# Columns of the second layer's scale and shift by transpositions, and 128 score columns for its first token tile

## The chip, the cores and the metric

The kernel runs on one core of one Trainium2 chip. The core has engines that run side by side: TensorE (PE, matrix products, with its weight loads PEld), VectorE (DVE), ScalarE (ACT), GpSimd (POOL), and SyncE (SP), which issues most of the transfers. The metric is the device time of one execution in microseconds, lower being better. Of several executions the median is given. The profile is of one more execution.

## What is computed

Two layers over 256 tokens of 1024 numbers, batch one. Each layer scales and shifts its normalized input by vectors that depend on a condition `c`, projects it, attends, gates the result and projects it back:

```python
cond = jax.nn.silu(c)
for i in range(DEPTH):
    shift, scale, gate = jnp.split(cond @ ada_w[i] + ada_b[i], 3, axis=-1)
    h = rms_norm(x, norm_g[i]) * (1 + scale[:, None, :]) + shift[:, None, :]
    ...
    x = x + gate[:, None, :] * y
```

The first layer's mixer (`nsa_mixer`) adds three attentions: over compressed blocks, over selected blocks and over a window. The second layer's (`moba_mixer`) is, at this length, plain causal attention, as its one block of 256 holds all tokens:

```python
s_own = jnp.einsum('bcgrd,bkgd->bcgrk', qc, k_own) * scale
...
p = masked_softmax(s_own, m_own).astype(v.dtype)
return jnp.einsum('bcgrk,bkgd->bcgrd', p, v_own)
```

There are 16 query heads of 64 and 4 key heads; a key head serves four query heads. All data are float32.

## The kernel before

**Products.** A weight or an activation is split in two fp32r parts, hi and lo, and a product is the sum of hi x hi, hi x lo and lo x hi, one pass each. The tokens are two tiles of 128 (`m` = 0 and 1). The normalized, scaled and shifted input stands transposed in `HT` (1024 features in eight groups of 128), so the scale and the shift are needed as columns, one number per partition and feature group: `AB[l]`.

**Scale and shift (`ada_rows`, `ada_ss`).** `ada_rows` multiplies the condition with the weights' columns. In `condz` only the first of each 32 columns holds the condition, the others are zero; four tiled products at a time put their results in PSUM rows 0 and 32 (the shift: even and odd feature groups of the condition) and 64 and 96 (the scale, likewise). All rows but these four are zero. The result is copied to `g` in SBUF, a tile "row". `ada_ss` turns these rows into columns and adds each pair: for each of the `nk` groups of 128 features, `g` is the stationary operand of a float32 product with `selP`, a 128x2 matrix with ones in rows 0 to 63 of its first column and in rows 64 to 127 of its second. Two additions and one fused step on VectorE then make `AB[l]`. The first layer does this in pieces of one or two groups (`nk` = 1, 2), the second layer in two pieces of four, which run as steps of the list `side` during the first layer's attention (`beside()` calls one step). The second layer's columns are first used in `next_h`, which makes the second layer's input after the first layer's output product.

**Second layer's attention (`pair_b`).** Eight pairs of heads. For each pair and each token tile `m`, `scores` computes two heads' scores against all 256 keys, keys split in hi and lo (`KTB`, a view of the tile KTA), with queries of one 128-token tile as the stationary operand: four products for each `m`. Of tile 0 only the first 128 keys are read by what follows (`masked_top`, which adds the causal mask and takes the row maximum); `exps`, the division, the transposition (`p_transposed`) and the product with the values follow, then `gated` with the `zT` columns.

**The order.** Nothing is issued as it stands in the code. `Plan` records each instruction, or each `plan.group()` of them, with what it reads and writes and a cost (`_cost`), and `issue` then simulates the engines and puts each engine's instructions in order by when they could start, by level (`FIRST_OF_ALL`, `URGENT`, `CHAIN`, `FILL`) and by which buffers are free. Tiles come from tags with a fixed number of buffers ("ps": six PSUM banks, "ss": four small SBUF tiles). Weight products are `FILL` and so stand between the attention's steps. PE's costs are in cycles, divided by 2.4 or 1.2 to get ns:

```python
if method == "transpose":
    return 262.0 if aps[1].dtype == F32 else 180.0
...
    return 2 * max(cols * 2.14, 264.0)
return max(cols * (1.07 if aps[2].dtype == F32R else 1.0), 264.0)
```

The third line is for a plain float32 product, the last for fp32r. As all instructions are issued from one place in `issue`, most rows of the profile show line L373; tile names tell them apart (`ps<-selP,row` is the product with `selP`, `ps<-KTA,qg` are scores, `row`, `AB` and `ss` are the tiles above).

Of the kernel before, what the change touches and what calls it, by code (L numbers as in the profile page):

```python
# [14 lines left out]
OP = mybir.AluOpType  # L15
AX = mybir.AxisListType

P = 128
# [382 lines left out]
def kernel(  # L401
# [29 lines left out]
    T, A, V, G, Q = plan.T, plan.A, plan.V, plan.G, plan.S  # L431
    tile_of = plan.tile
# [69 lines left out]
    identF = const.tile([P, P], F32, name="identF")  # L502
# [6 lines left out]
    selP = const.tile([P, 2], F32, name="selP")  # L509
# [130 lines left out]
    def ada_rows(l, cs, n, loaded=None):  # L640

        acc = tile_of("ps", 512)
        step = min(1024 // n, 4)
        level = plan.level if loaded else FILL
        for kk in range(8):
            if kk % step == 0:
                w = loaded[kk // step] if loaded else [ada_piece(l, kk, c0, n) for c0 in cs]
            run = max(step, 2) if n > P else 4
            if kk % run == run - 1:
                with plan.at(level), plan.group():  # L650
                    for k in range(kk - run + 1, kk + 1):
                        for s in range(2):
                            j = s * 2 + k % 2
                            T.matmul(acc[32 * j:32 * j + 32, :n], condz[:, k, :], w[s][:, k % step, :],
                                     start=(k < 2), stop=(k >= 6), tile_position=(0, 32 * j))
            if kk % step == step - 1 and kk < 7:
                yield
        g = tile_of("row", n)
        if n == P:
            V.tensor_copy(g, acc[:, :n])  # L660
        else:
            A.copy(g, acc[:, :n])
        return g
# [3 lines left out]
    def ada_ss(l, k0, nk, loaded=None):  # L667

        g = yield from ada_rows(l, (k0 * P, D + k0 * P), nk * P, loaded)
        t = tile_of("ps", 512)  # L670
        with plan.group():
            for q in range(nk):
                T.matmul(t[:, 2 * q:2 * q + 2], g[:, q * P:(q + 1) * P], selP, start=True, stop=True)
        tv = t[:, 0:2 * nk].rearrange("p (q s) -> p q s", s=2)
        b = ROW_ADA + 24 * l + k0
        a_, b_ = AB[l][:, 0, k0:k0 + nk], AB[l][:, 1, k0:k0 + nk]
        if nk == 1:
            V.tensor_scalar(a_, tv[:, :, 1], RT1[:, b + 8:b + 9], RT[:, ROW_G + 8 * l + k0:ROW_G + 8 * l + k0 + 1],
                            op0=OP.add, op1=OP.mult)
            V.tensor_add(b_, tv[:, :, 0], RT[:, b:b + nk])  # L680
            return
        V.tensor_add(a_, tv[:, :, 1], RT[:, b + 8:b + 8 + nk])
        V.scalar_tensor_tensor(a_, a_, 1.0, RT[:, ROW_G + 8 * l + k0:ROW_G + 8 * l + k0 + nk], op0=OP.add, op1=OP.mult)
        V.tensor_add(b_, tv[:, :, 0], RT[:, b:b + nk])
# [169 lines left out]
    def scores(q, kt, g, k0, n, need):  # L854

        s = tile_of("ps", 2, 256)
        with plan.group(need):
            for e in range(2):
                T.matmul(s[:, e, 0:n], q[e], kt[:, 0, g, k0:k0 + n], start=(e == 0), stop=False)
                T.matmul(s[:, e, 0:n], q[e], kt[:, 1, g, k0:k0 + n], start=False, stop=(e == 1))  # L860
        return s
# [4 lines left out]
    def masked_top(dst, src, neg, at):  # L866

        mask = causal[:, P - at:P - at + src.shape[-1]]
        V.tensor_tensor_reduce(dst, src, mask, -1.0, 3.0e38, op0=OP.add, op1=OP.min, accum_out=neg)

    def exps(dst, bias, total):
        A.activation(dst, dst, AF.Exp, bias=bias, scale=-1.0, accum_out=total)

    def inverse(sm):
        V.tensor_scalar_max(sm, sm, 1e-30)
        V.reciprocal(sm, sm)

    def p_transposed(block):

        pT = []  # L880
        for e in range(2):
            t = tile_of("ps", 512)
            with plan.group():
                for j in range(3):
                    T.transpose(t[:, j * P:(j + 1) * P], block(e, j), identF)
            s = tile_of("pT", 384)
            A.copy(s, t[:, 0:384])
            pT.append(s)
        return pT

    def values(o, parts, first):

        with plan.group():
            for n, (v, pT) in enumerate(parts):
                for e in range(2):
                    T.matmul(o[64 * e:64 * e + 64, 0:S], v[0], pT[e][:, 0:S], start=(first and n == 0), stop=False,
                             tile_position=(0, 64 * e))
                for e in range(2):
                    T.matmul(o[64 * e:64 * e + 64, P:S], v[1], pT[e][:, S:S + P], start=False,
                             stop=(n == len(parts) - 1), tile_position=(0, 64 * e))  # L900
# [3 lines left out]
    def gated(i, o, zT):  # L904
        t = tile_of("g", S)
        V.scalar_tensor_tensor(t, zT, 0.5, o[:, :S], op0=OP.mult, op1=OP.mult)
        if i % 2 == 0:
            pair = tile_of("qg", 2, 2, S)
            GT[i], GT[i + 1] = pair[:, 0], pair[:, 1]
        A.copy(GT[i][:, 0, :], t)  # L910
        V.tensor_sub(GT[i][:, 1, :], t, GT[i][:, 0, :].bitcast(F32))
# [53 lines left out]
    for m in range(2):  # L965
        xm, ss = tile_of("n_in", D), tile_of("ss", 16)[:, 0:1]
# [4 lines left out]
        for q in range(2):  # L971
            sl = slice(512 * q, 512 * q + 512)
            t = tile_of("ps", 4, P)
# [87 lines left out]
    for k in range(2):  # L1061
# [7 lines left out]
        with plan.at(URGENT):  # L1069
            for m in range(2):  # L1070
# [3 lines left out]
                h = tile_of("rot", P)  # L1074
# [6 lines left out]
        for m in range(2):  # L1081
            for ci, ((hi, lo), sl) in enumerate(w):
                acc = kv_acc[ci][m]
                with plan.at(FILL):
                    for i, (half, part) in enumerate(((0, hi), (0, lo), (1, hi))):
                        T.matmul(acc, HT[:, half, k, m * P:(m + 1) * P], part[:, sl],
                                 start=(k == 0 and i == 0 and (ci < 3 or m == 0)), stop=False, skip_group_check=True)

    for at, (what, k0, *rest) in enumerate(START):
        load_stage(what, k0, *rest)  # L1090
        if at == TABLES:
            TCS, NBc, TC, TR, TS = tables()
        if what == "s":
            nk = rest[0]
            with plan.at(URGENT):
                at_once(ada_ss(0, k0, nk, loaded[k0]))
                hv = xT[k0 // 4][:, k0 % 4:k0 % 4 + nk, :]
                for k in range(nk):
                    affine(HT[:, 0, k0 + k], hv[:, k, :], 0, k0 + k, A)
                    h = tile_of("rot", S)  # L1100
                    affine(h, hv[:, k, :], 0, k0 + k, V)
                    V.tensor_sub(HT[:, 1, k0 + k], h, HT[:, 0, k0 + k].bitcast(F32))
        else:
            for ci in range(4):
                w = parts_of(kv_w[k0][ci])
                for m in range(2):
                    product(kv_acc[ci][m], k0, m, w, of_h)
# [26 lines left out]
    for kv in range(2):  # L1134
        for m in range(2):
            t = tile_of("ps", 512)
# [3 lines left out]
            tv = t.rearrange("p (g u r e) -> p e r g u", g=KVH, r=8, e=2)  # L1140
# [22 lines left out]

    hid = tile_of("ps", 512)
    side += [cmp_steps(hid), ada_gate(0), ada_ss(1, 0, 4), ada_ss(1, 4, 4)]
    QT = qt_tiles()
    gates = const.tile([P, 2, HEADS, 3], F32, name="gates")
# [36 lines left out]
    with plan.group():  # L1204
        for cc in range(2):
            T.matmul(cmp_ps[0:64, 0:64], u[:, cc, 0, :], w2[:, 0, cc, :], start=(cc == 0), stop=(cc == 1))
        for m in range(2):
            T.matmul(cmp_ps[0:64, 64:96], selC[:, m].rearrange("p g n -> p (g n)"), TCS[:, m, :],
                     start=(m == 0), stop=(m == 1))
# [22 lines left out]
    for hf in range(2):  # L1232
        for cc in range(2):
# [4 lines left out]
                     start=(cc == 0), stop=(cc == 1))  # L1238
# [169 lines left out]
    KTB = KTA.rearrange("p a g k -> p (a g k)")[:, 0:2048].rearrange("p (a g k) -> p a g k", a=2, g=KVH)  # L1408
# [22 lines left out]
    def pair_b(i):  # L1431
        g = i // 2
        pm = [tile_of("p", 2, P), tile_of("p", 2, 256)]
        neg, sm = tile_of("tiny", 2, 2), tile_of("tiny", 2, 2)
        for m in range(2):
            n = P * (m + 1)
            q = [QT[g][:, 2 * (i % 2) + e, m * P:(m + 1) * P] for e in range(2)]
            s = scores(q, KTB, g, 0, 256, pm[m])
            for e in range(2):
                masked_top(pm[m][:, e], s[:, e, 0:n], neg[:, m, e:e + 1], m * P)  # L1440
            for e in range(2):
                exps(pm[m][:, e], neg[:, m, e:e + 1], sm[:, m, e:e + 1])
        inverse(sm.rearrange("p m e -> p (m e)"))
        for m in range(2):
            for e in range(2):
                V.tensor_scalar_mul(pm[m][:, e], pm[m][:, e], sm[:, m, e:e + 1])
        pT = p_transposed(lambda e, j: pm[0][:, e] if j == 0 else pm[1][:, e, (j - 1) * P:j * P])
        o = tile_of("ps", 512)
        vs = slice(g * HD, (g + 1) * HD)
        values(o, [([VB[:, m, vs] for m in range(2)], pT)], True)  # L1450
        gated(i, o, zT[i])

    for i in range(8):
        pair_b(i)
        beside()
# [37 lines left out]
```

## Time and profile before

| | |
|---|---|
| three runs, us | 319.18, 318.23, 319.22; median 319.18 |
| profiled execution, us | 318.98 |
| its span, first to last instruction, us | 317.3 |
| mean granted TensorE clock | 0.998 |
| HBM read | 64.36 MB |
| transfers' mean rate over the span | 207 GB/s |

How to read the profile: the page gives each engine's busy time and share of the span; "slices" cut the span into 40 parts, with the busy share in tenths. A group row has line, engine, operation, output and input tiles, shapes and count, then busy time in us and the mean length of one in ns, then idle time ahead of it. A timeline row has start, length, engine, the same names and a count, with idle time ahead of it in brackets. Records of PE overlap, since products are pipelined: a row's length is that of all its records together, from the first start to the last end. The chain of work that ended last is followed back from the end; its rows have start, length and what ran.

### The profile page before, as it was taken

The page shows a single profiled execution, that of the slowest core. Times are in us where ns is not written, and L with a number is a line of the kernel's source. Part 1 is how long each engine was busy: PE and PEld are TensorE (multiplying, and loading weights), DVE is VectorE, ACT ScalarE, POOL GpSimd, SP SyncE. Part 2 cuts the span into 40 slices and gives each one's busy share as a digit, 9 for nine tenths or more (in the row PEclk, how much of TensorE's full clock was granted, in tenths as well). Part 3 has the DMA queues.
Part 4 walks back from the last instruction along what each step waited for, and adds up shares of the span by engine and source line. Part 5 has one row for each costly group of instructions (what it writes and reads, how often), then busy time and mean ns, then how long its engine had stood idle before and what let it go on. Part 6 is the DMA issues. An engine that isn't in the chain of part 4 may idle for free.

```text
span 317.3 us, 6173 instructions
## 1 busy us (share of the span) xinstructions
PE 307.2 (97%) x2141; PEld 245.2 (77%) x2141; DVE 241.6 (76%) x732; ACT 205.2 (65%) x486; POOL 26.5 (8%) x102
## 2 busy tenths in 40 slices
PE   4999999999999999999999999999999999999995
PEld 4666677777766797868888988877788999968784
DVE  4663374669983899835979877997599999999763
ACT  5635155765835887456799856786586489998520
POOL 8138910000000000000000000000000000000000
PEclk9999999999999999999999999999999999999999
DMA  8999999359898813787274447727278872524002
GB/s 252 320 357 365 368 359 320 98 161 348 272 308 285 300 53 126 236 303 242 92 265 133 135 134 223 240 62 210 68 257 270 285 238 74 161 73 133 35 34 102
DMA packets 44174, 65.82 MB, mean 207 GB/s; under 512 B 4221, under 2 KB 20971, under 8 KB 44142
## 3 DMA queue, kind: packets, MB, share of 16 engines
q1 hardware_dynamic: 43782, 65.36, 63.8%
q8 instruction: 17, 0.28, 0.4%
q14 instruction: 15, 0.12, 0.1%
q10 hardware_dynamic: 168, 0.06, 0.1%
q0 software_dynamic: 192, 0.00, 0.0%
HBM read 64.36 MB, written 1.05 MB: 206 GB/s over the span
## 4 chain that ended last, share of the span: by engine, by line
PE 82%; DVE 7%; DMA 5%; ACT 3%; issue 2%; ACTq 0%; SPq 0%; DVEq 0%
PE ps L373 49%; PE acc L373 33%; DVE lo L373 3%; ACT hi L373 2%; DMA raw<-in_ada_w_dram 2%; DMA y<-in_ada_b_dram 2%; DMA early<-in_nsa_w_in_dram 1%; DVE n_out L373 1%; DVE gate L373 1%; DVE rs L373 0%; ACT n_in L373 0%; DVE p L373 0%; DVE ss L373 0%; DVE zT L373 0%; ACT p L373 0%
## 5 line engine op out<-in xcount | busy, mean ns | idle before, releaser
L373 DVE TENSOR_TENSOR lo<-raw,hi 128x1024 fp32r<-128x1024 f32 (+1 forms) x48 | 56.4, 1181 | 11.0 <-ACT hi L373 10.8
L373 ACT CAST hi<-raw 128x1024 fp32r<-128x1024 f32 (+1 forms) x48 | 48.9, 1022 | 23.1 <-DMA raw<-in_nsa_w_in_dram 8.3
L373 PE MATMUL acc<-hi,HT 128*128 128x512 f32 (+1 forms) x160 | 49.6, 381 | 1.5 <-ACT n_in L373 0.8
L373 ACT ACTIVATE p<-p,tiny 128x128 f32<-128x128 f32 (+1 forms) x96 | 43.0, 456 | 8.3 <-DVE tiny L373 8.2
L373 PE MATMUL acc<-HT,hi 128*128 128x256 f32 x192 | 37.7, 285 | 0.0
L373 PEld LDWEIGHTS acc<-hi,HT 128*128 128x128 f32 x160 | 29.0, 188 | 9.8 <-issue 2.9
L373 DVE CUSTOM_DVE_ANT_0 p<-ps,causal 128x128 f32<-128x128 f32 (+1 forms) x96 | 30.8, 345 | 3.5 <-PE ps L373 3.4
L373 PEld LDWEIGHTS acc<-HT,hi 128*128 128x128 f32 x192 | 30.1, 188 | 0.6 <-issue 0.6
L373 PE MATMUL acc<-lo,HT 128*128 128x512 f32 (+1 forms) x80 | 30.3, 380 | 0.2 <-DVE lo L373 0.2
L373 PE MATMUL ps<-hi,HT 128*128 128x512 f32 (+1 forms) x96 | 28.2, 365 | 0.0
L373 PE MATMUL acc<-HT,lo 128*128 128x256 f32 x96 | 27.7, 289 | 0.0
L373 PE MATMUL ps<-KTA,qg 128*128 128x256 f32 (+1 forms) x192 | 27.4, 286 | 0.0
L373 PEld LDWEIGHTS ps<-KTA,qg 128*128 128x128 f32 x192 | 24.4, 189 | 1.9 <-issue 1.5
L373 ACT COPY pT<-ps 128x384 f32<-128x384 f32 x48 | 21.5, 483 | 6.3 <-PE ps L373 6.1
L373 PE MATMUL ps<-hi,qg 128*128 128x256 f32 (+1 forms) x96 | 24.2, 322 | 0.0
L373 PE MATMUL acc<-hi,qg 128*128 128x512 f32 x64 | 23.1, 404 | 0.0
L373 PE MATMUL ps<-identF,p 128*128 128x128 f32 x144 | 21.7, 276 | 0.0
L373 PEld LDWEIGHTS ps<-hi,HT 128*128 128x128 f32 x96 | 17.0, 188 | 4.2 <-issue 2.1
L373 PEld LDWEIGHTS ps<-identF,p 128*128 128x128 f32 x144 | 16.4, 141 | 3.8 <-issue 1.2
L373 PE MATMUL ps<-pT,VA 128*64 128x256 f32 (+1 forms) x192 | 19.1, 334 | 0.0
L373 ACT ACTIVATION_READ_ACCUMULATOR p<-p,tiny 128x1 f32 x96 | 18.8, 196 | 0.0
L373 DVE TENSOR_SCALAR p<-p,tiny 128x256 f32<-128x256 f32 (+1 forms) x64 | 18.1, 329 | 0.0
(219 smaller groups left out, 616.5 us busy)
## 6 DMA issues: line engine op xcount, KB each, us to landing
raw<-in_ada_w_dram SPq DMA_DIRECT2D x32, 512.0 KB, 4.8
raw<-in_moba_w_in_dram SPq DMA_DIRECT2D x20, 512.0 KB, 4.7
early<-in_ada_w_dram SPq DMA_DIRECT2D x12, 512.0 KB, 9.5
raw<-in_nsa_w_in_dram SPq DMA_DIRECT2D x12, 512.0 KB, 6.0
early<-in_nsa_w_in_dram SPq DMA_DIRECT2D x9, 512.0 KB, 9.2
p<-in_nsa_cmp_w_dram SPq DMA_DIRECT2D x16, 256.0 KB, 4.1
raw<-in_nsa_w_out_dram SPq DMA_DIRECT2D x8, 512.0 KB, 5.2
raw<-in_moba_w_out_dram SPq DMA_DIRECT2D x8, 512.0 KB, 4.1
```

Source lines behind the costliest of these rows:

```text
L373: r = getattr(self.engines[e], method)(*[self._real(a) for a in args], **{k: self._real(a) for k, a in kw.items()})
```

## The change

Two places. In `ada_ss`, the second layer (`l` = 1) transposes each 128x128 part of `g` with the identity, in place of the product with `selP`, and VectorE sums each pair of columns that came from rows 0 and 32, and 64 and 96, into a small tile; the first layer stays as it was. In `pair_b`, token tile 0 computes scores against 128 keys, token tile 1 against 256 as before.

```diff
         with plan.group():
             for q in range(nk):
-                T.matmul(t[:, 2 * q:2 * q + 2], g[:, q * P:(q + 1) * P], selP, start=True, stop=True)
-        tv = t[:, 0:2 * nk].rearrange("p (q s) -> p q s", s=2)
+                if l:
+                    T.transpose(t[:, q * P:(q + 1) * P], g[:, q * P:(q + 1) * P], identF)
+                else:
+                    T.matmul(t[:, 2 * q:2 * q + 2], g[:, q * P:(q + 1) * P], selP, start=True, stop=True)
+        if l:
+            tv = tile_of("ss", nk, 2)
+            V.tensor_reduce(tv, t[:, 0:nk * P].rearrange("p (q s h z) -> p q s h z", q=nk, s=2, h=2)[:, :, :, :, 0],
+                            axis=AX.X, op=OP.add)
+        else:
+            tv = t[:, 0:2 * nk].rearrange("p (q s) -> p q s", s=2)
...
         for m in range(2):
             n = P * (m + 1)
             q = [QT[g][:, 2 * (i % 2) + e, m * P:(m + 1) * P] for e in range(2)]
-            s = scores(q, KTB, g, 0, 256, pm[m])
+            s = scores(q, KTB, g, 0, n, pm[m])
```

## What the change should do to the time

> **What bounds the kernel now.** I read the page first (busy shares, slices, chain), then the table of stretches, then the timeline of the two engines that the change touches.
>
> ```profile
> span 317.3 us, 6173 instructions
> PE 307.2 (97%) x2141; PEld 245.2 (77%) x2141; DVE 241.6 (76%) x732; ACT 205.2 (65%) x486; POOL 26.5 (8%) x102
> PEclk9999999999999999999999999999999999999999
> PE 82%; DVE 7%; DMA 5%; ACT 3%; issue 2%; ACTq 0%; SPq 0%; DVEq 0%
> ```
>
> TensorE (PE) is busy 97% of the span, holds 82% of the chain that ended last, and its granted clock never falls below nine tenths. So a nanosecond of PE's issue time is worth about a nanosecond, unless it is saved just ahead of one of the few places where PE really waits. The stretches that the change touches, or whose work comes after it:
>
> ```profile
> 138.00:165.00 27.00, 27.00 (x238) 21.56 (x236) 18.77 (x98) 20.76 (x71) 0.00 (x0) 1.00 0.61 202
> 205.00:230.00 25.00, 24.75 (x112) 18.75 (x111) 19.19 (x44) 17.32 (x40) 0.00 (x0) 1.00 0.41 122
> 230.00:257.00 27.00, 26.88 (x181) 24.36 (x179) 26.55 (x50) 17.95 (x24) 0.00 (x0) 1.00 0.85 271
> 257.00:302.00 45.00, 44.96 (x346) 38.23 (x347) 41.64 (x155) 37.83 (x110) 0.00 (x0) 1.00 0.34 106
> ...
> PE ps L373 <- DVE n_parts L373: 0.2, 1, 0.2
> PE ps L373 <- ACT n_in L373: 0.2, 1, 0.2
> ```
>
> The columns are length, then busy time of PE, weight load, DVE, ACT, POOL, then clock, DMA share and GB/s. The first row holds both transposition groups, the last one all second-layer scores. PE is full in both, at clock 1.00. DVE is full in 230 to 257 (26.55 of 27.00) and nearly so behind it (41.64 of 45.00). The two lower rows, from the list of waits, are all of PE's idle time after 130 us. PE's busy time is no measure of what an instruction costs, as records overlap: I use distances between starts.
>
> **The change part by part.** First the two selP groups of the second layer.
>
> ```profile
> 138.51 0.49 PE L373 MATMUL ps<-identF,p 128*128 128x128 f32 x3
> 138.84 0.99 PE L373 MATMUL ps<-selP,row 128*128 128x2 f32 x8
> 139.76 0.44 PE L373 MATMUL ps<-pT,VA 128*64 128x256 f32 x2
> ...
> 160.68 0.95 PE L373 MATMUL ps<-selP,row 128*128 128x2 f32 x8
> 161.50 1.18 PE L373 MATMUL ps<-identF,p 128*128 128x128 f32 x9
> ...
> 265.33 0.82 PE L373 MATMUL ps<-identF,p 128*128 128x128 f32 x6
> ...
> L373 PE MATMUL ps<-identF,p 128*128 128x128 f32 x48 | 6.9, 272 | 0.0
> ```
>
> Four products make eight records: a plain f32 product runs as two. The groups hold PE from 138.84 to 139.76 (0.92 us) and from 160.68 to 161.50 (0.82 us), 1.74 us together. A transposition of a 128x128 f32 tile is one record: six of them in a row last 0.82 us, of which the last is 272 ns long, so the step is (0.82 - 0.272) / 5 = 0.110 us. Four make 0.44 us. The first group is 0.10 us longer than the second, and a tiled product follows it (64 columns wide, a change of mode); I put the 0.10 us down to that change and keep it. So 0.92 becomes 0.54, 0.82 becomes 0.44: **saved 0.38 + 0.38 = 0.76 us**. This is an exactly known kind of instruction, so I put it at 0.7 to 0.8.
>
> The sums over two rows, which the product with selP did on the way, go to DVE: one reduction of 16 elements to 8 per group, ahead of the two additions and the fused step that there were.
>
> ```profile
> 139.87 0.23 DVE L373 TENSOR_TENSOR AB<-ps,RT 128x4 f32<-128x4 f32 x2 [1.46 <-PE ps L373]
> 140.06 0.16 DVE L373 SCALAR_TENSOR_TENSOR AB<-AB,RT 128x4 f32<-128x4 f32 x1
> 141.33 0.42 DVE L373 SCALAR_TENSOR_TENSOR g<-zT,ps 128x256 f32<-128x256 f32 x1 [1.10 <-PE ps L373]
> ...
> 164.04 0.29 DVE L373 CUSTOM_DVE_ANT_0 p<-ps,causal 128x128 f32<-128x128 f32 x1 [2.01 <-PE ps L373]
> ...
> L373 DVE TENSOR_REDUCE emask<-identF 128x8 f32<-128x128 f32 x1 | 0.5, 467 | 0.0
> L373 DVE TENSOR_REDUCE ss<-kcy 64x1 f32<-64x64 f32 x1 | 0.2, 208 | 0.0
> L373 DVE TENSOR_TENSOR AB<-ps,RT 128x4 f32<-128x4 f32 x4 | 0.5, 157 | 1.6 <-PE ps L373 1.5
> ```
>
> No row reduces 16 elements; the nearest are 467 ns for 128 elements, 208 ns for 64, and 157 ns for the additions. I take 0.2 us, between 0.15 and 0.47. Behind the first group DVE's next instruction waits 1.10 us for PE, behind the second it is idle 2.01 us before 164.04: both reductions lie in that idle time, and I cost them at nothing. If that cover were gone, they would be 0.4 us of DVE, in a stretch where DVE has 8 of 27 us free. The reduction waits for the same PE group as the additions did, and the group ends earlier; what stands behind it on DVE is the gating of the next pair, which waits for PE anyway. The additions then read SBUF; 157 ns is the floor of so small an instruction either way. The columns are first used by next_h behind 205 us, over 40 us later. No transfer is added. The new tile needs one of the four "ss" buffers for under a microsecond, where the two "squares" tiles aren't yet in use, and the PSUM bank comes free earlier.
>
> Second, the scores of token tile 0: 8 pairs, 2 heads, 2 parts (hi, lo) make 32 records of 64.
>
> ```profile
> L373 PE MATMUL ps<-KTA,qg 128*128 128x256 f32 x64 | 9.1, 285 | 0.0
> 258.75 2.53 PE L373 MATMUL ps<-KTA,qg 128*128 128x256 f32 x20
> ...
> L373 PE MATMUL ps<-KTA,qg 128*128 128x32 f32 x32 | 3.9, 263 | 0.0
> 123.76 1.60 PE L373 MATMUL ps<-KTA,qg 128*128 128x32 f32 x13
> ...
> L373 PE MATMUL ps<-identR,n_parts 128*128 128x128 f32 x32 | 3.2, 247 | 0.2 <-DVE n_parts L373 0.2
> 257.04 1.56 PE L373 MATMUL ps<-identR,n_parts 128*128 128x128 f32 x16 [0.17 <-DVE n_parts L373]
> ...
> L373 PE MATMUL ps<-pcT,Vbd 128*128 128x256 f32 x12 | 3.5, 390 | 0.0
> 162.51 1.03 PE L373 MATMUL ps<-pcT,Vbd 128*128 128x256 f32 x4
> ```
>
> Twenty of these scores in a row give (2.53 - 0.285) / 19 = 0.118 us each. The same kind of product with 32 columns, the compressed scores, gives (1.60 - 0.263) / 12 = 0.111. An eighth of the columns saves 6%: something other than the columns sets the step. Each record has a weight load of its own (PE and PEld count 2141 each on the page), which points at that load. A product of 128 columns isn't in the trace. From below: fp32r transpositions with 128 columns, (1.56 - 0.247) / 15 = 0.088. From above: the rate of plain f32, (1.03 - 0.390) / 3 = 0.213 per record of 256 columns, two records a product, so 0.213 for a whole product of 128 columns. I take 0.111, the nearest in kind (same tiles, same weights). **Saved 32 x 0.007 = 0.22 us**; the ends are 32 x 0.030 = 0.96 us saved and 32 x 0.095 = 3.04 us lost.
>
> The Trainium skill has a rule that speaks against this half of the change: in "TensorE: Matmul & The Clock Gate", section "LDWEIGHTS (loading the stationary operand)", a weight load takes its number of columns divided by 1.2, in ns, which for 128 is 107 ns however few columns stream past. The 32-column row agrees (0.111 measured). By that rule alone the scores would save 32 x (0.118 - 0.107) = 0.35 us as an estimate, in place of my 0.22.
>
> Third, the order. Every instruction is put in order by the planner from its own costs, and the change alters these: a two-column f32 product costs 528 cycles there, a transposition 262, so each group shrinks from 2112 to 1048 cycles, at its divisor of 2.4 from 0.88 to 0.44 us, close to what the trace has. Each score shrinks from 273.9 to 264 cycles, 4 ns. Two DVE instructions are new. All that follows 138 us can so be interleaved differently. I cost that at nothing, as PE is filled by weight products in any order, with about 0.1 us lost at each change between whole and tiled products; some ten such changes more or fewer are 1 us, the size of the whole effect.
>
> The sum: -0.76 - 0.22 = **-0.98 us**. The profiled execution took 318.98 us (span 317.3 and 1.7 around it), so 318.0; the median of the three runs is 319.18, and 0.98 below it is 318.2. I forecast 318.1. What a measurement of this kernel can tell from no change is about 0.3%, 0.96 us: the forecast lies on that line.
>
> **The rivals.**
>
> (a) The gain is swallowed on the way. PE waits at two places behind the first groups:
>
> ```profile
> 205.85 0.40 PE L373 MATMUL ps<-lo,qg 128*128 128x512 f32 x1
> 206.41 0.44 PE L373 MATMUL ps<-identF,n_in 128*128 128x128 f32 x2 [0.16 <-ACT n_in L373]
> ...
> 216.34 12.87 PE acc L373 x54
> 229.23 1.06 ACT hi L373
> 237.13 5.01 DMA raw<-in_ada_w_dram
> 256.38 0.61 DVE n_parts L373
> ```
>
> At 206 it waits for the scaled X of the second layer, at 257 for DVE's queries. If what ends there isn't moved by PE, the 0.76 us turns into a longer wait, and only the 0.22 us is left: 318.98 - 0.2 = 318.8. For it: the chain (last four rows) leaves PE at 229.23 and runs through DVE and a 5.01 us transfer up to 257, with DVE full. Against it: both chains start at a PE product (the 12.87 us ahead of 229.23), so they start earlier by as much.
>
> (b) Slower: fp32r products with fewer than 256 columns fall to the plain f32 rate. Place: the 32 narrow scores, 257 to 302 us, where PE is full. Price: +3.04 us, less 0.76: 318.98 + 2.28 = 321.3. It decides as soon as a narrow score's step passes 0.118 + 0.76 / 32 = 0.142 us. Against it: plain f32 products make two records, and the 32-column scores are one record each at 0.111 us; but at the f32 rate 32 columns would stream in a quarter of 0.213, which the load would hide, so it isn't excluded. The fp32r transpositions of 128 columns step at 0.088, under plain f32's 0.110, which speaks against a fall too, for another mode.
>
> (c) The new order is worse where DVE is full.
>
> ```profile
> L373 DVE TENSOR_TENSOR lo<-raw,hi 128x1024 fp32r<-128x1024 f32 (+1 forms) x48 | 56.4, 1181 | 11.0 <-ACT hi L373 10.8
> ```
>
> If the new order puts two more weight splits ("lo", 1.18 us each) ahead of the queries between 230 and 257, PE waits that much longer at 257: 2.36 - 0.98 = +1.38 us, 320.4. For it: PE already waits for DVE there. Against it: the planner sees that stretch with costs that the change doesn't touch.
>
> (d) The narrow scores step like the fp32r transpositions: -0.96 - 0.76 = -1.72, so 317.3. For it speaks only the 0.088 row; the weight load of 0.111 in the 32-column row speaks against. The Trainium skill, "TensorE: Matmul & The Clock Gate", section "Back-to-back issue gap", gives about 81 ns for a sustained stream of loads and products with 128 columns, which would be this rival.
>
> **How the numbers follow.** Gain carried, as forecast, 317.6 to 318.6: 0.50, of it 0.30 past the line and 0.20 short of it. (a) 318.6 to 319.4: 0.22, no change. (b) 321.3: 0.10, slower. (c) 319.9 to 320.8: 0.10, slower. (d) 317.0 to 317.5: 0.08, faster. So faster 0.38, within 0.3% 0.42, slower 0.20. The range goes from 317.0, the end of (d), to 321.3, that of (b), since both ends of the unknown score step belong in it; the likeliest case's own range is 317.6 to 318.6.
>
> **What would show it.** Right: two groups of four transpositions that hold PE 0.44 to 0.54 us, no selP records behind 130 us, reductions in DVE's idle time, and 32 scores of 128 columns with steps near 0.111. Wrong: steps of the narrow scores at 0.2 us (b) or 0.09 (d); waits of PE around 206 and 257 that have grown by 0.7 us (a); a span that moves by over 1 us while both PE savings stand, which is order (c).

## The result and the profile after

The changed kernel took 317.09 us (median of 7 runs, 315.94 to 317.45), the kernel before 318.62 us (7 runs, 317.80 to 319.78). The ratio is 0.9942, with a 95% interval of 0.9919 to 0.9966; in a second comparison it was 0.9947 (0.9929 to 0.9966). So the change saves 0.5 to 0.6%, some 1.7 to 1.8 us (the medians differ by 1.5 us). The forecast had the sign, 318.1 us and 0.98 us of gain, with "within 0.3%" as the likeliest class; the gain is clear of that line.

The page of the changed kernel, with the lines that answer to those shown of before:

```profile
span 315.7 us, 6158 instructions
PE 306.0 (97%) x2133; PEld 243.5 (77%) x2133; DVE 242.2 (77%) x734; ACT 205.0 (65%) x486; POOL 26.6 (8%) x102
PEclk9999999999999999999999999999999999999999
PE 90%; DMA 5%; ACT 2%; DVE 1%; issue 1%; SPq 0%; ACTq 0%; DVEq 0%
```

PE has eight records fewer (2133 for 2141: sixteen for selP became eight transpositions), DVE two more. PE is still the bound, with 90% of the chain for 82%. The timeline of the two groups in the changed kernel, PE first, then DVE:

```profile
138.60 0.49 PE L373 MATMUL ps<-identF,p 128*128 128x128 f32 x3
138.93 0.60 PE L373 MATMUL ps<-identF,row 128*128 128x128 f32 x4
139.46 0.65 PE L373 MATMUL ps<-pT,VA 128*64 128x256 f32 x4
...
160.44 0.60 PE L373 MATMUL ps<-identF,row 128*128 128x128 f32 x4
160.88 1.15 PE L373 MATMUL ps<-identF,p 128*128 128x128 f32 x9
...
139.57 0.17 DVE L373 TENSOR_REDUCE ss<-ps 128x8 f32<-128x16 f32 x1 [1.06 <-PE ps L373]
141.03 0.42 DVE L373 SCALAR_TENSOR_TENSOR g<-zT,ps 128x256 f32<-128x256 f32 x1 [0.89 <-PE ps L373]
161.25 0.17 DVE L373 TENSOR_REDUCE ss<-ps 128x8 f32<-128x16 f32 x1
163.41 0.29 DVE L373 CUSTOM_DVE_ANT_0 p<-ps,causal 128x128 f32<-128x128 f32 x1 [1.59 <-PE ps L373]
```

The groups hold PE for 139.46 - 138.93 = 0.53 us and 160.88 - 160.44 = 0.44 us, where the forecast had 0.54 and 0.44. A reduction takes 0.17 us, and behind it and the three small steps that use it DVE is idle (0.89 and 1.59 us): the reductions lie in idle time. The narrow scores, by the group row for 130 us to the end and the timeline:

```profile
L373 PE MATMUL ps<-KTA,qg 128*128 128x128 f32 x32 | 4.3, 267 | 0.0
276.17 1.08 PE L373 MATMUL ps<-KTA,qg 128*128 128x128 f32 x8
```

(The eight of the second row are four narrow and four wide scores, merged.) In the trace, the step from one narrow score to the next has a median of 0.111 us, the value taken from the 32-column row.

So every term that was priced came out near its price, and the total is off by almost as much again. To see where, I cut each execution at the same PE records: the three transpositions ahead of the first group (138.51 us in before), the scores behind the second group (163.19), a product of the first layer's output (187.61), a weight product 22 records ahead of the queries' transpositions (254.22), the first score of the second layer (258.44), the last product (313.30), and the end. The work between two of them is the same in all kernels but for the edited instructions, by a count of the records. Three executions of before and two of the changed kernel, lengths in us between the starts of those records:

| stage from, us of before | 0 | 138.5 | 163.2 | 187.6 | 254.2 | 258.4 | 313.3 to end | 138.5 to end |
|---|---|---|---|---|---|---|---|---|
| before | 138.51 | 24.68 | 24.42 | 66.61 | 4.22 | 54.86 | 3.96 | 178.75 |
| before, second | 137.57 | 24.67 | 24.42 | 66.61 | 4.10 | 55.02 | 4.13 | 178.96 |
| before, third | 137.28 | 24.67 | 24.43 | 66.61 | 4.04 | 55.02 | 4.03 | 178.80 |
| changed | 138.60 | 23.94 | 24.20 | 66.59 | 4.05 | 54.52 | 3.85 | 177.14 |
| changed, second | 137.00 | 23.87 | 24.20 | 66.60 | 4.03 | 54.52 | 3.85 | 177.06 |

The first column is the same code in all five, and differs by 1.6 us; the last column differs by 0.2 within a kernel and by 1.7 between them. So the scatter of the total lies ahead of the change, and from 138.5 us on the gain is 1.7 us: 0.77 in the stage with the groups, 0.22 in the next, 0.3 to 0.5 in the second layer's attention, and, taking means, 0.1 around 257 us and 0.2 at the end.

### The profile page after: what moved, and what is told of

It reads as the page before. It is cut to its first block, busy times and chain, and to the rows that moved or that the text cites. A ratio compares the mean times of both kernels' runs of the same rounds, so it can differ in the third digit from the quotient of the medians.

```text
span 315.7 us, 6158 instructions
## 1 busy us (share of the span) xinstructions
PE 306.0 (97%) x2133; PEld 243.5 (77%) x2133; DVE 242.2 (77%) x734; ACT 205.0 (65%) x486; POOL 26.6 (8%) x102
## 3 DMA queue, kind: packets, MB, share of 16 engines
HBM read 64.36 MB, written 1.05 MB: 207 GB/s over the span
## 4 chain that ended last, share of the span: by engine, by line
PE 90%; DMA 5%; ACT 2%; DVE 1%; issue 1%; SPq 0%; ACTq 0%; DVEq 0%
PE ps L373 54%; PE acc L373 36%; DMA raw<-in_nsa_w_in_dram 2%; DMA early<-in_ada_w_dram 2%; ACT hi L373 1%; DMA rot<-in_c_dram 0%; ACT n_in L373 0%; DVE lo L373 0%; DVE p L373 0%; ACT p L373 0%; DVE AB L373 0%; ACT HT L373 0%; DVE rot L373 0%; DVE y L373 0%; DVE X L373 0%
## 5 line engine op out<-in xcount | busy, mean ns | idle before, releaser
L373 PE MATMUL ps<-KTA,qg 128*128 128x256 f32 (+2 forms) x192 | 27.0, 284 | 0.0
L373 PEld LDWEIGHTS acc<-HT,lo 128*128 128x128 f32 x96 | 18.1, 189 | 0.1
```

Of the source, the lines that this page charges most:

```text
L373: r = getattr(self.engines[e], method)(*[self._real(a) for a in args], **{k: self._real(a) for k, a in kw.items()})
```

## The experiments

Each of the first four is compared with the kernel before in five rounds, all on one chip. Together they cross two things: the instructions, old or new, and the order in which the planner puts them, old or new.

**Transpositions alone.** Scores stay at 256 columns:

```diff
-            s = scores(q, KTB, g, 0, n, pm[m])
+            s = scores(q, KTB, g, 0, 256, pm[m])
```

> The transpositions alone, all scores with 256 columns, order as the planner makes it. Theory A (the two PE savings of the forecast hold, and the new order adds about 0.5 us, 0.2 of it between 165 and 187 us and 0.2 by the wait at 257 us that is gone): 1.2 us under before, PE ahead of before by 0.8 us behind the second group. Theory B (order is worth nothing, what is over the forecast is scatter): 0.8 us under. Theory C (the narrow scores are worth more than their step, as VectorE can start earlier): 0.8 us under.

Measured: ratio 0.9973 (0.9954 to 0.9992), 317.70 us for 318.18. By stages: 23.94, 24.20, 66.57, 4.18, 54.87, 3.85, together 177.60, 1.24 us under the mean of the three executions of before (178.84). That is theory A's number, but in part by chance: 0.1 to 0.3 of it are in the last stage, which A did not have, and A's 0.2 at 257 us isn't there (4.18 for 4.04 to 4.22). The stage with the groups gives 0.74, the next, which has no changed instruction, 0.22.

**Narrow scores alone.** The kernel before with only the second part of the change:

```diff
-            s = scores(q, KTB, g, 0, 256, pm[m])
+            s = scores(q, KTB, g, 0, n, pm[m])
```

> The 128-column scores alone; the second layer's rows still go through the product with selP. Theory A: 0.2 to 0.3 us under before, no lead of PE ahead of 257 us. Theory B: 0.2 us under. Theory C: 0.8 us under, all of it behind 257 us.

Measured: ratio 0.9979 (0.9951 to 1.0008), which does not exclude that nothing changed. By stages: 24.68, 24.42, 66.61, 4.03, 54.52, 3.84, together 178.12: 0.72 under. Ahead of 254 us it is before's to 0.01 us. The attention has 54.52, as in the changed kernel, 0.34 to 0.50 under before: more than theory A's 0.2 to 0.3. By this run alone, theory C (0.8 us, all behind 257 us) is nearer; the next one decides. The stage around 257 has 4.03 without any change ahead of it, and before's third execution has 4.04: PE's wait there comes and goes.

**New instructions, old order.** The planner counts the new instructions with the costs and the reads of the old ones:

```diff
+            turn["cost"] = nk * 528.0
...
+            with plan.group() as op:
+                V.tensor_reduce(tv, t[:, 0:nk * P].rearrange("p (q s h z) -> p q s h z", q=nk, s=2, h=2)[:, :, :, :, 0],
+                                axis=AX.X, op=OP.add)
+                V.tensor_add(a_, tv[:, :, 1], RT[:, b + 8:b + 8 + nk])
+            op["cost"] = 1.042 * nk + 68.0
...
+        op["cost"] = 4 * 256 * 1.07
+        for part in range(2):
+            plan._touch(op, kt[:, part, g, k0:k0 + 256], False)
```

> The changed instructions in the order of before: transpositions, reductions and 128-column scores, but the planner counts them with the costs and the reads of the old ones, so that every engine's order is that of before. Theory A: 1.0 us under before, PE's lead constant at 0.8 us from the second group to 257 us. Theory B: as the changed kernel, within 0.2 us of it. Theory C: 1.5 us under, with over 0.6 us gained behind 257 us.

Measured: ratio 0.9955 (0.9939 to 0.9971), 317.15 us for 318.18. By stages: 23.89, 24.69, 66.56, 4.05, 54.74, 3.85, together 177.78: 1.06 under, theory A's number again. The ratio doesn't tell this kernel from the changed one (0.9942 and 0.9947); the stages do, with 177.78 for 177.06 and 177.14, so theory B, which had the two within 0.2 us, falls by these. From 130 us on, PE and ACT go through their work in before's order in this trace, but for the edited records. The narrow scores are here without their new order, and the attention takes 54.74, only 0.1 to 0.3 under before: theory C, with over 0.6, falls. But the way to it isn't A's: the lead was not constant. Of the 0.79 us won by the groups, 0.27 is lost by 187 us. PE's timeline of this kernel, then of before, then of the changed kernel:

```profile
164.67 1.21 PE L373 MATMUL ps<-KTA,qg 128*128 128x256 f32 x8
165.71 0.49 PE L373 MATMUL ps<-identF,p 128*128 128x128 f32 x3
165.96 0.60 PE L373 MATMUL acc<-HT,hi 128*128 128x256 f32 x3
166.44 0.55 PE L373 MATMUL ps<-identF,p 128*128 128x128 f32 x3
167.21 0.87 PE L373 MATMUL ps<-identF,p 128*128 128x128 f32 x6 [0.23 <-ACT pT L373]
167.92 0.60 PE L373 MATMUL ps<-pcT,Vbd 128*128 128x256 f32 x2
```

```profile
165.39 1.21 PE L373 MATMUL ps<-KTA,qg 128*128 128x256 f32 x8
166.43 0.49 PE L373 MATMUL ps<-identF,p 128*128 128x128 f32 x3
166.68 0.60 PE L373 MATMUL acc<-HT,hi 128*128 128x256 f32 x3
167.12 1.29 PE L373 MATMUL ps<-identF,p 128*128 128x128 f32 x9
168.28 0.70 PE L373 MATMUL ps<-pcT,Vbd 128*128 128x256 f32 x2
```

```profile
164.75 1.23 PE L373 MATMUL ps<-KTA,qg 128*128 128x256 f32 x8
165.81 0.82 PE L373 MATMUL ps<-identF,p 128*128 128x128 f32 x6
166.38 0.60 PE L373 MATMUL acc<-HT,hi 128*128 128x256 f32 x3
166.87 0.88 PE L373 MATMUL ps<-identF,p 128*128 128x128 f32 x6
167.58 0.60 PE L373 MATMUL ps<-pcT,Vbd 128*128 128x256 f32 x2
```

All three do eight scores, twelve transpositions and three weight products. In the old order, three transpositions stand ahead of the weight products and nine behind. A PE that comes 0.7 us earlier then finds the PSUM bank of the nine not yet emptied by ACT's copy (`pT`): a wait of 0.23 us, and 167.92 - 164.67 = 3.25 us for the piece, where before took 168.28 - 165.39 = 2.89. The new order has six ahead and six behind: 167.58 - 164.75 = 2.83, no wait. The order of ACT has its part in this too. Its rows of the same piece, in this kernel and then in the changed one:

```profile
165.73 1.05 ACT L373 CAST hi<-raw 128x1024 fp32r<-128x1024 f32 x1
166.66 0.50 ACT L373 COPY pT<-ps 128x384 f32<-128x384 f32 x1
...
166.10 0.21 ACT L373 ACTIVATION_READ_ACCUMULATOR p<-p,tiny 128x1 f32 x1
166.34 0.86 ACT L373 COPY pT<-ps 128x384 f32<-128x384 f32 x2
```

In the old order a weight cast of 1.05 us stands right ahead of the first copy, which ends at 166.66 + 0.50 = 167.16; PE's fourth transposition starts at 167.21. In the new order the cast isn't there. Before has the cast too (its copy ends at 167.48), and waits there a little already: its nine transpositions take 168.28 - 167.12 = 1.16 us, where nine steps of 0.110 are 0.99. Which part of the wait is the cast's and which that of three and nine transpositions in place of six and six, no run tells.

**Old instructions, new order.** The product with selP, a copy of its result and 256-column scores, but planned as if they were the new ones:

```diff
+            op["cost"] = nk * 262.0
+            tv = tile_of("ss", nk, 2)
+            op = V.tensor_copy(tv, t[:, 0:2 * nk].rearrange("p (q s) -> p q s", s=2))
...
+        if wide:
+            op["calls"] = [("matmul", (s[:, e, 0:256], q[e], kt[:, part, g, k0:k0 + 256]),
+                            {"start": e + part == 0, "stop": e + part == 2}) for e in range(2) for part in range(2)]
```

> The old instructions in the order of the changed kernel: the product with selP and a copy of its result in place of the transpositions and the reduction, scores with 256 columns, but counted by the planner as the new ones. Theory A: 0.5 us under before, none of it ahead of 165 us, 0.2 us by 187 us, 0.2 us more at 257 us. Theories B and C: as before, within 0.2 us.

Measured: ratio 0.9978 (0.9962 to 0.9993), 317.83 us for 318.18. By stages: 24.68, 24.14, 66.60, 4.23, 54.79, 3.85, together 178.29: 0.55 under, as theory A had it. 0.28 of it comes between 163 and 187 us; theories B and C, by which the order alone is worth nothing, fall. A's 0.2 at 257 us isn't there (4.23); 0.1 to 0.2 come in the attention in its place, and 0.1 to 0.3 in the last stage. Most of the 0.28 is the piece shown above, from one set of scores to the next. In before, then in this kernel:

```profile
163.19 0.82 PE L373 MATMUL ps<-KTA,qg 128*128 128x256 f32 x4
168.63 0.47 PE L373 MATMUL ps<-KTA,qg 128*128 128x256 f32 x1
...
162.73 0.82 PE L373 MATMUL ps<-KTA,qg 128*128 128x256 f32 x4
167.99 0.58 PE L373 MATMUL ps<-KTA,qg 128*128 128x256 f32 x2
```

That is 5.44 us for 5.26, so 0.18; the other 0.10 is spread over the rest of the stage in parts too small to put down to anything. What the order does in the attention, by the timeline of before and then of the changed kernel:

```profile
287.62 0.87 PE L373 MATMUL ps<-pT,VA 128*64 128x256 f32 x8
288.42 0.74 PE L373 MATMUL ps<-KTA,qg 128*128 128x256 f32 x4
289.09 0.87 PE L373 MATMUL ps<-pT,VA 128*64 128x256 f32 x8
```

```profile
285.11 1.08 PE L373 MATMUL ps<-KTA,qg 128*128 128x128 f32 x8
286.03 0.49 PE L373 MATMUL ps<-identF,p 128*128 128x128 f32 x3
```

In before, four scores stand between two tiled value products: they hold PE for 289.09 - 288.42 = 0.67 us, 0.2 more than four steps of 0.118, one change of mode on each side. In the new order the eight scores of the pair stand together, 286.03 - 285.11 = 0.92 us, without a neighbour of that kind. But that isn't 0.2 us won: by a count of the records PE changes between whole and tiled products 16 times in the attention and 8 times between 163 and 187 us, in the old order and in the new, so other records stand next to the tiled ones instead.

What the order is worth in the attention is smaller than the stages suggest. There the step from one weight product `acc<-HT` to the next has a mean of 114.2 ns in before's first execution, of 116.4 in its other two and of 116.2 in the kernel with the old order, and of 113.9 to 114.3 in this kernel and the changed one (of the steps from 105 to 125 ns, 64 in each). Over these, 2.2 ns are 0.14 us, which is what before's executions differ by (54.86 and 55.02). Where the steps are alike, the new order is worth 54.86 - 54.79 = 0.07 us. Whether it also sets the step isn't known: the step is short in all five profiles with the new order there, and in two of the five with the old. The narrow scores can be priced in the same way: this kernel and the changed one have the same order and nearly the same step, and differ by 54.79 - 54.52 = 0.27 us.

**The two kernels once more.** The second profiles in the table above are from these.

> The changed kernel once more. If PE's progress from 133 us on is the same in every execution: 0.79 us won by the two groups, 0.2 more by 187 us, 0.3 more behind 258 us, as in its first profile. If the wait at 257 us is gone because of the change, it is gone here too.

> The kernel before once more. If the wait at 257 us belongs to its order, it is here with 0.15 to 0.2 us; if it is scatter of the transfers ahead of it, it can be absent. The wait at 78 us should differ from the first profile's 0.78 us by some tenths, as it does among the experiments, which have the same code up to there.

> The kernel before a third time, with the same expectation: PE's wait at 257 us is there each time if it belongs to the order of before, and comes and goes if it is scatter; the wait at 78 us varies by some tenths.

Measured: the changed kernel has ratio 0.9947 (0.9929 to 0.9966); its stages repeat to 0.1 us. PE's wait for the queries at 257 us is absent in both its profiles, but the list of PE's waits of before's third execution, from 60 us on, doesn't have it either:

```profile
PE acc L373 <- ACT n_in L373: 0.6, 1, 0.6
PE ps L373 <- DVE p L373: 0.3, 1, 0.3
PE ps L373 <- ACT n_in L373: 0.2, 1, 0.2
```

No line names DVE n_parts. So it is scatter, with a size of up to 0.2 us, and no part of the change's gain can be put down to it. The wait at 78 us (the first line, 0.6 here) was 0.8 in before's first profile and is missing in its second.

**The first layer too.** The changed kernel, with transpositions also in the first layer's three groups of two:

```diff
-                if l:
+                if l or nk > 1:
```

> The changed kernel, with the first layer's three groups of two products turned into transpositions and a reduction too. Each group holds PE for four records of 0.11 us before and two after. Theory A (PE time saved is time saved wherever PE is full): 3 x 0.2 = 0.6 us under the changed kernel. Rival (in the first 60 us the group stands in a chain that ends in VectorE's columns and waits for transfers, and the reduction lengthens it): the same as the changed kernel or up to 0.5 us over it, and whatever PE wins by 57 us is lost in the wait for the raw weights at 78 us.

Measured: 317.51 us, ratio to before 0.9986 (0.9961 to 1.0011), where the changed kernel in the same comparison has 316.99 us and 0.9947. From 138.5 us on it is the changed kernel (177.10 us in all); its gain was to come ahead of that. Counted at equal work and against before, PE wins 0.3 us at the first group (27 us) and 0.5 us at the other two together (40 and 51 us). Its list of waits between 14 and 90 us, and then that of before:

```profile
PE ps L373 <- DVE p L373: 0.6, 1, 0.6
PE acc L373 <- ACT n_in L373: 0.3, 1, 0.3
PE acc L373 <- ACT HT L373: 0.3, 1, 0.3
PE acc L373 <- DVE lo L373: 0.2, 1, 0.2
```

```profile
PE acc L373 <- ACT n_in L373: 0.8, 1, 0.8
PE ps L373 <- DVE p L373: 0.3, 1, 0.3
PE acc L373 <- DVE lo L373: 0.2, 1, 0.2
```

The wait for ACT's HT is new, and at 30 us the first group's gain is gone. The wait for DVE's p at 63 us doubles, and behind it, at 64 us, PE is 0.2 us behind before again. So the rival is right that PE isn't the bound there, but not about the place: it had the loss at 78 us, where the wait for n_in is shorter here than in before's first profile, by scatter. The interval of the total is wide enough that a small loss or gain stays open; it is no better than the changed kernel.

## Why the prediction was right and wrong

- **What bounds the kernel.** Right from 138 us on, with one exception: the 0.77 us that PE wins in the group stage is still there at the end, but in the old order 0.27 of it goes into a wait for ACT. It was too broad for the first 80 us, as the first-layer experiment shows.
- **The two groups, 0.76 us.** Right: 0.74 to 0.81 us in each of the five executions that have them.
- **The reductions, nothing.** Right: 0.17 us each, in DVE's idle time.
- **The scores, 0.22 us.** Right, if a little small: the step is 0.111, and in one and the same order they are worth 54.79 - 54.52 = 0.27 us.
- **The order, "I cost that at nothing".** This step failed. The new order alone, with the old instructions, is worth 0.55 us from 138.5 us on (0.4 without the last stage), with ratio 0.9978; 0.28 of it lies between 163 and 187 us and 0.07 in the attention. With the new instructions, the stage from 163 to 187 us takes 24.69 us in the old order and 24.20 in the new. The reason given, that weight products fill PE in any order and only some ten changes of mode matter, does not hold in either half: the number of changes stayed the same, and transpositions wait for PSUM banks that ACT has to empty, so that the order of two engines counts. The planner's new costs are no truer than its old ones (0.88 us for a group that took 0.82 to 0.92, 0.44 for one that takes 0.44 to 0.53), and the fourth experiment gained under costs that aren't those of its instructions. So no run shows why the new order came out better; as far as these runs go, that it helped is luck.
- **The sum and its place on the line.** From 138.5 us on 1.74 us are gained, 0.76 more than forecast. The groups are 0.77 of it, the scores 0.27, and the order 0.22 between 163 and 187 us, where in the old order 0.27 would have been lost, and 0.07 in the attention: about 1.3 us. The rest can't be put down to the change. 0.1 is the longer step of the weight products in two of before's executions, 0.1 the wait at 257 us, which comes and goes, and 0.2 the last 4 us. These are 3.84 to 3.85 us in all profiles but those of before (3.96 to 4.13), by one transfer: the last output transfer is issued 1.23 us behind the start of the last product in every profile, and lands 3.05, 3.22 and 3.11 us behind it in before's, and 2.93 to 2.94 in the others. Why isn't known.
- **The rivals.** (a) did not come: both chains start at PE, and the lead at 187 us is still there at 254. (b) fell: 128-column fp32r products step at 0.111, with no fall to plain f32's rate. (c) had the order as a cost, but with the wrong sign and in another place: between 187 and 254 us nothing moved (66.59 for 66.61), and the wait at 257 us didn't grow. (d) fell as well: no 0.088 either. The rule of the Trainium skill on weight loads ("TensorE: Matmul & The Clock Gate", "LDWEIGHTS (loading the stationary operand)") agrees with 32 and 128 columns having one step, 0.111 us for its 107 ns. The 81 ns that the Trainium skill gives for 128 columns in the section "Back-to-back issue gap" of the same page don't hold for these products, with their 0.111 us.
- **The chances.** The largest, 0.42, was on no change, as the priced terms came to the line itself; the order, unpriced, entered only as the loss of (c). The measured 317.09 us lies within the 317.0 to 317.5 of (d), but not by the way of (d), since no score steps at 0.088. The forecast did name the sign of what came, a span that moves by over 1 us while both savings on PE stand; it had put it down to a worse order.

## What to carry to other kernels

Where a scheduler works from costs, an edit changes two things, the instructions and the order, and each can be measured by itself: plan with one set of costs and issue the other. Cut executions at the same records ahead of and behind the edit; here that turned a scatter of 1.6 us in the total into 0.2 us. A product with few columns is paid for by a step that they don't shorten (0.111 us for 32 and for 128), so halving 256 columns bought 0.27 us over 32 products, while halving the records of eight (a plain f32 product against a transposition) bought 0.77.

## What the runs showed of the hardware

The step of an fp32r product is 0.111 us for 32 and for 128 columns and 0.117 for 256. At the borders of such a run the steps differ: in the eight scores at 276.17 us the second narrow one starts 0.06 us behind the first, and the second wide one 0.17 us behind the first wide one, while the steps within each kind are 0.11 and 0.12. The eight together hold PE for 277.09 - 276.17 = 0.92 us: a single step at a border says nothing, the sum does.
